# Last tiles in groups of 256, 128 and 128 tokens, a lane for the MLP's weight sums, and a block inverse in two halves

## The chip, the cores and the metric

One core of a Trainium2 chip runs the whole kernel: TensorE (PE) multiplies, VectorE (DVE), ScalarE (ACT) and GpSimd (POOL) do the rest, SyncE (SP) and ScalarE issue the transfers. The metric is device time in microseconds. Each engine works off its own queue in order; an instruction waits there for the data or the buffer it needs, and what stands behind it waits too.

## The reference

Two layers over 512 tokens of width 1024, in float32. Each is `x += mixers(rmsnorm(x) @ w_in) @ w_out` with four mixers (retention, a gated linear recurrence, latent attention, gated DeltaNet), then cross attention on a memory, then the MLP. A final norm ends it:

```python
h = rmsnorm(x, norm_mlp[l])
x = x + jnp.square(jax.nn.relu(h @ mlp_w1[l])) @ mlp_w2[l]
...
return rmsnorm(x, final_norm)
```

The DeltaNet mixer solves a unit lower triangular system of 64 x 64 per chunk and head:

```python
sol = lax.linalg.triangular_solve(lower + jnp.eye(c, dtype=F32), rhs,
                                  left_side=True, lower=True, unit_diagonal=True)
```

## The kernel before

`x` stays on the chip, transposed: eight tiles `xr[m]` of 128 features by 512 tokens. Nearly every large product is split into three: a factor is rounded to a float32r high part (`...h`) by ScalarE, VectorE subtracts to get the low part (`...l`), and PE adds high by high, high by low and low by high in PSUM.

A scheduler orders each engine's queue by a running priority number; `lane(key, base)` (line 212) issues what is inside it with a priority counted on from `base`, or from where that lane was left. The in-projection and the four mixers run in such lanes, from `(2l+1)*1e7 + 1e5` on; what follows the mixers starts at `(2l+1)*1e7 + 5e6` (`end`, line 536). PSUM has two banks under `pj`, two under `gd`, three under `ch` and one under `lg`.

**Weights** come through `wload` (line 276), one unit ahead of another as buffers permit. Most are loaded as `wr` and split into `wh` and `wl`. The units of the MLP's first matrix are treated otherwise: it is multiplied block by block with seven products instead of eight, on sums and differences of its blocks. `wload` brings the four raw blocks (`sr`, two buffers), POOL forms four combinations (`sm`, two buffers), ScalarE rounds three raw blocks (`ah`) and the combinations (`wh`), VectorE makes the low parts `al` (128 x 768, line 299) and `wl` (128 x 1024, line 303). `al` and `wl` have two buffers each, `ah` and `wh` three. Raw buffer `sr` is free once the sums, `ah` and `al` have read it.

**The MLP** combines the normed input in the same way: `prep` forms block differences of `hp`, on VectorE for the last index and on POOL for others, and `combo` splits them into `cxh` and `cxl` (VectorE, line 234). `sprod` (line 1520) runs a weight unit against them in two passes (`dj`), 21 matmuls of 256 columns in each; a pass begins with products on `ah` and `al`, then come those on `wh` and `wl`. Of the first eighth of the hidden width all four units are run, then second-matrix units are interleaved; each fills four PSUM banks, which `evac` (line 1574) empties: VectorE multiplies by the token scale into `t_` (two buffers), POOL adds `t_` to `x`.

**The block inverse** (lines 739 to 790, in the lane `GDN`) inverts 16 pairs of 64 x 64 blocks. VectorE transposes 32-row blocks (lines 763, 764) and four products of 32 small matmuls (`tiles`) follow, each into a `gd` bank; what lies between is a masked product on VectorE, ScalarE copies and two transposes (line 782). Projection matmuls (`pj`) stand between in PE's queue.

**The last tiles** (`last_tiles`, line 1317) end the second layer: the final four feature tiles m = 4 to 7 are computed for two groups of 256 tokens, 12 matmuls each. `tile` adds to `x`, squares it and accumulates; `rstd_of` sums over features with one-column matmuls, `rsqrt1` takes the root (ScalarE, then VectorE with one correction step); `finish` broadcasts the result over the partitions through PE (`bc`) and multiplies eight tiles, five on VectorE and three on POOL, each followed by its output transfer, on ScalarE's queue for odd m and on SP's for even m.

Of the kernel before, what the change touches and what calls it, by code (L numbers as in the profile page):

```python
# [20 lines left out]
S = 512  # L21
# [159 lines left out]
def build(tc, A, out, dbg=None):  # L181
# [10 lines left out]
    def nm(s):  # L192
        uid[0] += 1
        return f"{s}_{uid[0]}"
# [82 lines left out]
    def wload():  # L277
# [7 lines left out]
        if PLAN[i][2][2] is None:  # L285
            sw = wstate["sw"]
            raw = sw.tile([128, n], F32, tag="sr", name=nm("sr"), bufs=2)
            SP.dma_start(out=raw, in_=A["wu"][off:off + 128 * n].rearrange("(p n) -> p n", p=128))
            sm = sw.tile([128, 1024], F32, tag="sm", name=nm("sm"), bufs=2)
            a11, a12, a22, a21 = (raw[:, j * 256:j * 256 + 256] for j in range(4))  # L290
            s1, s3, s2, s4 = (sm[:, j * 256:j * 256 + 256] for j in range(4))
            tt(G, s1, a21, a22, AD)
            tt(G, s2, s1, a11, SU)
            tt(G, s4, a12, s2, SU)
            tt(G, s3, a11, a21, SU)
            ah = sw.tile([128, 768], F32R, tag="ah", name=nm("ah"), bufs=3)
            al = sw.tile([128, 768], F32R, tag="al", name=nm("al"), bufs=2)
            act(ah, raw[:, 0:768], AF.Copy)
            tt(V, al, raw[:, 0:768], ah.bitcast(F32), SU)
            hi = wp.tile([128, n], F32R, tag="whi", name=nm("wh"), bufs=3)  # L300
            lo = wp.tile([128, n], F32R, tag="wlo", name=nm("wl"), bufs=2)
            act(hi, sm, AF.Copy)
            tt(V, lo, sm, hi.bitcast(F32), SU)
            wstate["tiles"][u] = (ah, al, hi, lo)
            return
# [70 lines left out]
    def rsqrt1(o, v, n):  # L376
        w = tiny.tile([128, n], F32, tag=f"rw{n}", name=nm("rw"))
        nv = tiny.tile([128, n], F32, tag=f"rn{n}", name=nm("rn"))
# [54 lines left out]
    def rstd_of(acc, ntt=TT, root=rsqrt, new=None):  # L433
# [5 lines left out]
        v = tiny.tile([128, ntt], F32, tag=f"rv{ntt}", name=nm("rv"))  # L439
        ts(V, v, ps[:, 0:ntt], 1.0 / D, MU, EPS, AD)  # L440
        r = tiny.tile([128, ntt], F32, tag=f"rstd{ntt}", name=nm("rstd"))
# [85 lines left out]
    def layer(l):  # L527
# [111 lines left out]
        def gdn_pre():  # L639
# [121 lines left out]
            for q in range(4):  # L761
                rw, cb = slice(32 * q, 32 * q + 32), slice(32 * (q % 2), 32 * (q % 2) + 32)
                V.transpose(U3[rw, :, cb].rearrange("p t (f r) -> p r f t", f=2), Us3[rw])
                V.transpose(Ta[rw, :, cb], U3[rw, :, cb])
            ps = sct()
            tiles(sb4(ps), N3, cut4(Ta)[:, :, :, 0, :])
            tt(V, cut4(PI)[:, :, :, 0, :], sb4(ps),
               C("zm").unsqueeze(1).unsqueeze(3).to_broadcast([128, 16, 2, 16]), MU)
# [5 lines left out]
            ps = sct()  # L774
            tiles(sb4(ps), PI, cut4(U3)[:, :, :, 1, :])
            act(cut4(U3)[:, :, :, 1, :], sb4(ps), AF.Copy)
# [3 lines left out]
            for p in range(2):  # L780
                ra = slice(64 * p, 64 * p + 32)
                V.transpose(Tb3[ra], U3[ra, :, 0:32])
            ps = sct()
            tiles(sb3(ps), N3, Tb3)
            for p in range(2):
                rb = slice(64 * p + 32, 64 * p + 64)
                act(P1[rb, :, 0:32], sb3(ps)[rb], AF.Copy)
            ps = sct()
            tiles(sb3(ps), P1, U3[:, :, 32:64])
            act(U3[:, :, 32:64], sb3(ps), AF.Copy)  # L790
# [526 lines left out]
        def last_tiles(facc, hh, hl, r2):  # L1317
            ws = [wnext("w27bk0"), wnext("w27ck0")]
            rs, sqs = {}, [None]
            parts = lambda g: [facc[:, g * 256:g * 256 + 256], sqs[0][:, 0:256], sqs[0][:, 256:512]]  # L1320

            def tile(g, m):
                s = slice(g * 256, g * 256 + 256)
                wh, wl = ws[(m - 4) // 2]
                ps = cyb()[:, 0:256]
# [3 lines left out]
                t_ = mp.tile([128, S], F32, tag="t_", name=nm("th"), bufs=2)[:, 0:256]  # L1329
# [3 lines left out]
                sq = sqs[0][:, 256:512] if m == 7 else sqs[0][:, 0:256]  # L1333
# [7 lines left out]
            def finish(g):  # L1341
                s = slice(g * 256, g * 256 + 256)
                b, bp = bcast(rs[g], 256, mp, True)
# [7 lines left out]
            for m in range(4, 8):  # L1351
                tile(0, m)
            p0 = parts(0)
            tile(1, 4)
            rs[0] = rstd_of(p0, 2, rsqrt1)
            tile(1, 5)
            tile(1, 6)
            tile(1, 7)
            rs[1] = rstd_of(parts(1), 2, rsqrt1)
            finish(0)  # L1360
            finish(1)

# [368 lines left out]
```

## Time and profile before

| what | value |
|---|---|
| median of 3 runs | 1622.28 us (1620.12 to 1623.71) |
| the profiled execution's own time | 1620.33 us |
| its span | 1618.5 us |
| PE busy | 1574.2 us, 97% of the span |
| DVE busy | 1134.7 us, 70% |
| ACT busy | 784.2 us, 48% |
| POOL busy | 502.2 us, 31% |
| granted PE clock, mean | 0.992 of full speed |

The span runs from the first to the last instruction of the one profiled execution. Busy shares are means over stages that differ; starts in a timeline are counted from the start of the span. PEclk is the granted TensorE clock as a share of 2.4 GHz, so 0.5 is 1.2 GHz. In a timeline row the number in brackets is the idle time before the instruction and what ended it. A plain float32 matmul appears as two records, a float32r one as one.

### The profile page before, as it was taken

The page shows a single profiled execution, that of the slowest core. Times are in us where ns is not written, and L with a number is a line of the kernel's source. Part 1 is how long each engine was busy: PE and PEld are TensorE (multiplying, and loading weights), DVE is VectorE, ACT ScalarE, POOL GpSimd, SP SyncE. Part 2 cuts the span into 40 slices and gives each one's busy share as a digit, 9 for nine tenths or more (in the row PEclk, how much of TensorE's full clock was granted, in tenths as well). Part 3 has the DMA queues.
Part 4 walks back from the last instruction along what each step waited for, and adds up shares of the span by engine and source line. Part 5 has one row for each costly group of instructions (what it writes and reads, how often), then busy time and mean ns, then how long its engine had stood idle before and what let it go on. Part 6 is the DMA issues. An engine that isn't in the chain of part 4 may idle for free.

```text
span 1618.5 us, 25948 instructions
## 1 busy us (share of the span) xinstructions
PE 1574.2 (97%) x10094; PEld 1366.5 (84%) x10094; DVE 1134.7 (70%) x2197; ACT 784.2 (48%) x1269; POOL 502.2 (31%) x473
## 2 busy tenths in 40 slices
PE   9999999999999999999999999999999899999997
PEld 7768898888888998889886788988888889999886
DVE  7887786456577666766787968745576777766665
ACT  5655654344454444444445656434355544444434
POOL 0100000201274566665301000002014665565543
PEclk9999999999999999999999999999999999999998
DMA  5211125332213223232331212253322223232321
GB/s 184 76 52 54 46 74 167 129 116 80 91 66 105 102 94 97 99 104 66 124 117 48 66 41 75 94 168 117 105 65 92 92 92 104 93 105 93 104 66 65
DMA packets 48074, 150.81 MB, mean 93 GB/s; under 512 B 5712, under 2 KB 9808, under 8 KB 47952
## 3 DMA queue, kind: packets, MB, share of 16 engines
q1 hardware_dynamic: 46800, 148.12, 27.8%
q8 instruction: 79, 1.29, 0.3%
q10 hardware_dynamic: 1152, 1.05, 0.2%
q14 instruction: 43, 0.35, 0.1%
HBM read 144.95 MB, written 4.19 MB: 92 GB/s over the span
## 4 chain that ended last, share of the span: by engine, by line
PE 74%; DVE 13%; issue 4%; ACT 3%; POOL 3%; DMA 3%; SPq 0%; POOLq 0%; DVEq 0%; ACTq 0%
PE ch L249 25%; PE pj L249 23%; PE gd L249 18%; PE lg L249 7%; DVE wl L234 2%; DMA wr<-in_wu 2%; POOL hp L234 1%; PE ch L454 1%; ACT wh L246 1%; POOL sm L234 1%; POOL acc L234 1%; DVE x L234 1%; DMA mem<-in_memT 1%; DVE Pm L241 0%; ACT hp L246 0%
## 5 line engine op out<-in xcount | busy, mean ns | idle before, releaser
L234 DVE TENSOR_TENSOR wl<-wr,wh 128x1024 fp32r<-128x1024 f32 (+2 forms) x193 | 257.5, 1334 | 228.8 <-issue 74.1
L246 ACT ACTIVATE wh<-wr 128x1024 fp32r<-128x1024 f32 (+2 forms) x193 | 201.4, 1044 | 252.9 <-DMA wr<-in_wu 74.8
L249 PE MATMUL ch<-hp,wh 128*128 128x512 f32 (+1 forms) x768 | 238.4, 392 | 0.9 <-DVE hp L234 0.9
L234 POOL TENSOR_TENSOR sm<-sr 128x256 f32<-128x256 f32 x128 | 99.7, 800 | 343.4 <-PE pj L249 133.4
L249 PEld LDWEIGHTS ch<-hp,wh 128*128 128x128 f32 x768 | 140.4, 189 | 29.3 <-DVE hp L234 1.5
L249 PE MATMUL ch<-hp,wl 128*128 128x512 f32 (+1 forms) x384 | 150.4, 392 | 0.0
L234 POOL TENSOR_TENSOR acc<-acc,sq 128x512 f32<-128x512 f32 x33 | 52.9, 1603 | 299.5 <-ACT sq L246 299.5
L246 ACT ACTIVATE wh<-sm 128x1024 fp32r<-128x1024 f32 x64 | 67.4, 1053 | 124.9 <-PE lg L249 110.7
L234 DVE TENSOR_TENSOR al<-sr,ah 128x768 fp32r<-128x768 f32 x64 | 89.4, 1397 | 50.4 <-PE gd L249 50.3
L246 ACT ACTIVATE W<-W 128x1024 f32<-128x1024 f32 x64 | 67.7, 1059 | 80.0 <-DVE W L234 79.1
L249 PE MATMUL pj<-wl,xh 128*128 128x256 f32 (+1 forms) x352 | 106.5, 303 | 0.0
L249 PE MATMUL pj<-wh,xl 128*128 128x256 f32 (+1 forms) x352 | 104.5, 297 | 0.0
L249 PE MATMUL pj<-wh,xh 128*128 128x256 f32 (+1 forms) x352 | 103.0, 293 | 1.4 <-DVE gd L237 1.3
L249 PE MATMUL pj<-cxh,wl 128*128 128x256 f32 x360 | 102.5, 285 | 0.4 <-DVE wl L234 0.4
L249 PE MATMUL pj<-cxh,wh 128*128 128x256 f32 x360 | 102.1, 284 | 0.0
L249 PE MATMUL pj<-cxl,wh 128*128 128x256 f32 x360 | 101.4, 282 | 0.0
L249 PEld LDWEIGHTS ch<-hp,wl 128*128 128x128 f32 x384 | 72.4, 189 | 16.1
L234 DVE TENSOR_TENSOR wl<-sm,wh 128x1024 fp32r<-128x1024 f32 x64 | 80.3, 1254 | 4.0 <-PE gd L249 2.9
L249 PE MATMUL lg<-hp,wh 128*128 128x512 f32 (+1 forms) x256 | 78.9, 390 | 0.0
L246 ACT ACTIVATE ah<-sr 128x768 fp32r<-128x768 f32 x64 | 53.9, 846 | 49.3 <-PE gd L249 37.2
L249 PE MATMUL gd<-cxh,al 128*128 128x256 f32 x240 | 68.4, 285 | 6.2 <-DVE al L234 6.2
L249 PEld LDWEIGHTS pj<-wh,xh 128*128 128x128 f32 x352 | 67.6, 192 | 2.9 <-DVE gd L237 1.8
(789 smaller groups left out, 4673.4 us busy)
## 6 DMA issues: line engine op xcount, KB each, us to landing
wr<-in_wu SPq DMA_DIRECT2D x183, 512.0 KB, 3.4
sr<-in_wu SPq DMA_DIRECT2D x64, 512.0 KB, 3.4
x<-in_xT SPq DMA_DIRECT2D x16, 256.0 KB, 4.0
wr<-in_wu SPq DMA_DIRECT2D x8, 360.0 KB, 2.9
mem<-in_memT SPq DMA_DIRECT2D x16, 128.0 KB, 3.0
xs<-x SPq DMA_DIRECT2D x8, 256.0 KB, 2.3
x<-xs SPq DMA_DIRECT2D x8, 256.0 KB, 2.7
big<-in_wmla SPq DMA_DIRECT2D x2, 640.0 KB, 4.6
```

The lines of the kernel that those rows point to most:

```text
L234: e.tensor_tensor(o, a, b, op=op)
L246: ACT.activation(o, i, f, **k)
L249: PE.matmul(o, lhsT=l, rhs=r, start=st, stop=sp, **k)
L454: PE.transpose(o, i, ident)
```

## The change

Three parts. `wload` puts everything that it does for a unit of the MLP's first matrix into a lane of its own, whose numbers begin where those of the layer's later half begin, so that these instructions go ahead of all others of that half once they are issued. The block inverse runs each of its four products as two halves of eight blocks, each with its own 256-column half bank, and its transposes of line 764 and 782, its ScalarE copies and its masked product in halves too. The last tiles run in token groups of 256, 128 and 128; the middle group has four of its eight closing products on POOL.

```diff
         if PLAN[i][2][2] is None:
+            with lane(f"sw{l}", (2 * l + 1) * 10000000 + 5000000):
+                sw = wstate["sw"]
...
-            def tiles(o, l_, r_):
-                for a in range(16):
+            def tiles(o, l_, r_, h):
+                for a in range(8):
                     for p in range(2):
                         rw = slice(64 * p, 64 * p + 64)
-                        mm(o[rw, a], l_[rw, a, :], r_[rw, a], True, True)
+                        mm(o[rw, a], l_[rw, 8 * h + a, :], r_[rw, 8 * h + a], True, True)
+            def open_(h):
+                for q in range(4):
+                    rw, cb = slice(32 * q, 32 * q + 32), slice(32 * (q % 2), 32 * (q % 2) + 32)
+                    if h == 0:
+                        V.transpose(U3[rw, :, cb].rearrange("p t (f r) -> p r f t", f=2), Us3[rw])
+                    V.transpose(Ta[rw, HV[h], cb], U3[rw, HV[h], cb])
+            def two_(h):
+                ps = sct()[:, 0:256]
+                tiles(sb4(ps), PI, cut4(U3)[:, :, :, 1, :], h)
+                act(cut4(U3)[:, HV[h], :, 1, :], sb4(ps), AF.Copy)
+                for p in range(2):
+                    ra = slice(64 * p, 64 * p + 32)
+                    V.transpose(Tb3[ra, HV[h]], U3[ra, HV[h], 0:32])
...
+            open_(0)
+            one(0)
+            open_(1)
+            one(1)
...
+            for f, h in ((two_, 0), (two_, 1), (three, 0), (three, 1), (four, 0), (four, 1)):
+                f(h)
...
+            GR = ((0, 256), (256, 128), (384, 128))
...
-                    if m in (2, 5, 7):
+                    if m in ((2, 5, 7), (1, 3, 5, 7), (2, 5, 7))[g]:
...
+            for g in range(3):
+                p = parts(g - 1) if g else None
+                tile(g, 4)
+                if g:
+                    root(g - 1, p)
+                for m in range(5, 8):
+                    tile(g, m)
+                if g == 2:
+                    root(2, parts(2))
+                if g:
+                    finish(g - 1)
+            finish(2)
```

The scheduler turns the first part into a few moves. At the opening of the first MLP VectorE's queue stood like this, from the accumulation of squares (`acc`) on; `hp` and `cxl` are the combinations of the input and their low parts, the first `al` and `wl` are of the MLP's fourth unit, the next two of the fifth:

```order
L234 TENSOR_TENSOR acc_4545<-acc_4545,sq_5118 128x512
L234 TENSOR_TENSOR hp_4884<-hp_4883,hp_4884 128x256
L234 TENSOR_TENSOR cxl_4907<-hp_4883,cxh_4906 128x512
L234 TENSOR_TENSOR hp_4884<-hp_4883,hp_4884 128x256
L234 TENSOR_TENSOR cxl_4909<-hp_4883,cxh_4908 128x256
L234 TENSOR_TENSOR cxl_4911<-hp_4884,cxh_4910 128x512
L234 TENSOR_TENSOR al_4934<-sr_4926,ah_4933 128x768
L234 TENSOR_TENSOR cxl_4913<-hp_4884,cxh_4912 128x512
L234 TENSOR_TENSOR wl_4938<-sm_4928,wh_4937 128x1024
L234 TENSOR_TENSOR al_4995<-sr_4987,ah_4994 128x768
L234 TENSOR_TENSOR wl_4999<-sm_4989,wh_4998 128x1024
```

The first `al` stood behind five operations on the input. In the changed kernel, at the same place, VectorE's queue is:

```order
L234 TENSOR_TENSOR acc_4560<-acc_4560,sq_5133 128x512
L234 TENSOR_TENSOR al_4949<-sr_4941,ah_4948 128x768
L234 TENSOR_TENSOR hp_4899<-hp_4898,hp_4899 128x256
L234 TENSOR_TENSOR cxl_4922<-hp_4898,cxh_4921 128x512
L234 TENSOR_TENSOR wl_4953<-sm_4943,wh_4952 128x1024
L234 TENSOR_TENSOR hp_4899<-hp_4898,hp_4899 128x256
L234 TENSOR_TENSOR cxl_4924<-hp_4898,cxh_4923 128x256
L234 TENSOR_TENSOR cxl_4926<-hp_4899,cxh_4925 128x512
L234 TENSOR_TENSOR cxl_4928<-hp_4899,cxh_4927 128x512
L234 TENSOR_TENSOR al_5010<-sr_5002,ah_5009 128x768
L234 TENSOR_TENSOR wl_5014<-sm_5004,wh_5013 128x1024
```

`al` moved to the place behind `acc`, and `wl` ahead of four operations; POOL's queue and PE's are the same here. At the first evacuation of the first MLP VectorE's queue held, from the token scale (`r`) on, four products `t_`, one for each PSUM bank, and then the weights:

```order
L234 TENSOR_TENSOR r_1076_5415<-bc_5413 128x512
L234 TENSOR_TENSOR t__1077_5417<-ch_5279,r_1076_5415 128x512
L234 TENSOR_TENSOR t__1078_5420<-ch_5280,r_1076_5415 128x512
L234 TENSOR_TENSOR t__1079_5423<-ch_5281,r_1076_5415 128x512
L234 TENSOR_TENSOR t__1080_5426<-lg_5282,r_1076_5415 128x512
L234 TENSOR_TENSOR wl_5445<-sm_5435,wh_5444 128x1024
L234 TENSOR_TENSOR al_5532<-sr_5524,ah_5531 128x768
```

The four products stood together. In the changed kernel the weights stand among them on VectorE:

```order
L234 TENSOR_TENSOR r_1080_5430<-bc_5428 128x512
L234 TENSOR_TENSOR t__1081_5432<-ch_5294,r_1080_5430 128x512
L234 TENSOR_TENSOR al_5547<-sr_5539,ah_5546 128x768
L234 TENSOR_TENSOR t__1082_5435<-ch_5295,r_1080_5430 128x512
L234 TENSOR_TENSOR wl_5460<-sm_5450,wh_5459 128x1024
L234 TENSOR_TENSOR t__1083_5438<-ch_5296,r_1080_5430 128x512
L234 TENSOR_TENSOR t__1084_5441<-lg_5297,r_1080_5430 128x512
```

`al` now goes ahead of the second product and `wl` ahead of the third; on POOL two of the four additions of `t_` stand behind three and four sums. This is the only place in an MLP where POOL's queue differs. In layer 0 PE's queue at the second and third product of the inverse (`gd_894`, `gd_932`; `ch` belongs to the attention) was:

```order
L249 MATMUL gd_894<-g_140_841,g_138_799 64x32 x32
L249 MATMUL ch_1491<-bf_194_1229,bf_192_1227 128x256
L454 MATMUL ch_1503<-cst,o_274_1483 128x128 x2
L249 MATMUL ch_1472<-o_276_1489,bf_196_1231 128x128
L249 MATMUL pj_2100<-wl_1980,xh_126 128x256
L249 MATMUL pj_2100<-wh_1979,xl_134 128x256
L249 MATMUL pj_2100<-wh_1979,xh_127 128x256
L249 MATMUL pj_2100<-wl_1980,xh_127 128x256
L249 MATMUL pj_2100<-wh_1979,xl_135 128x256
L249 MATMUL gd_932<-g_145_928,g_132_741 64x32
```

Between the two products stood five projection matmuls and three groups of the attention. In the changed kernel PE's queue has, for the halves of the first (`gd_877`), second (`gd_902`, `gd_922`) and third product (`gd_942`, `gd_961`):

```order
L249 MATMUL gd_877<-g_141_843,g_132_741 64x32
L249 MATMUL gd_902<-g_140_841,g_138_799 64x32 x12
L249 MATMUL gd_877<-g_141_843,g_132_741 64x32 x15
L249 MATMUL gd_902<-g_140_841,g_138_799 64x32 x4
L456 MATMUL ch_1502<-cst,o_270_1479 128x128
L249 MATMUL pj_2115<-wl_1995,xh_126 128x256
L249 MATMUL pj_2115<-wh_1994,xl_134 128x256
L249 MATMUL pj_2115<-wh_1994,xh_127 128x256
L249 MATMUL gd_922<-g_140_841,g_138_799 64x32 x16
L249 MATMUL gd_942<-g_145_900,g_132_741 64x32 x16
L249 MATMUL ch_1506<-bf_198_1244,bf_196_1242 128x256
L249 MATMUL gd_961<-g_145_900,g_132_741 64x32
```

Halves of one product and of the next now stand side by side, and the projection matmuls that stood between them have moved behind. In the last tiles PE's queue has 48 matmuls of 256 columns and 96 of 128 instead of 96 of 256; each group's fourth-tile matmuls stand ahead of the root of the group before. On ScalarE's queue the four transfers of the first group stand ahead of the middle group's square root, and three of the middle group's transfers ahead of the last `bc`.

## Rows read from the trace of the kernel before

**Rows 1.** TensorE's waits: engine, line, releaser, us in total, times, longest
```profile
PE gd L249 <- DVE al L234: 6.2, 2, 3.1
PE gd L249 <- DVE g L764: 3.4, 2, 1.8
```

**Rows 2.** Windows: stretch, length, busy time by engine, PEclk, DMA share, GB/s
```profile
469.60:473.00 3.40, 3.37 (x16) 3.37 (x17) 3.40 (x4) 0.00 (x0) 0.00 (x0) 0.51 0.44 154
926.98:933.80 6.82, 6.82 (x95) 6.53 (x93) 4.58 (x11) 1.73 (x3) 2.25 (x4) 0.51 0.03 9
```

**Rows 3.** Timeline, TensorE, MLP openings: start, us, engine, line, tiles, form, wait
```profile
466.11 0.28 PE L249 MATMUL gd<-cxh,ah 128*128 128x256 f32 x1
466.23 0.28 PE L249 MATMUL gd<-cxl,ah 128*128 128x256 f32 x1
...
469.63 0.58 PE L249 MATMUL gd<-cxh,al 128*128 128x256 f32 x1 [3.12 <-DVE al L234]
...
473.44 0.28 PE L249 MATMUL gd<-cxh,ah 128*128 128x256 f32 x1
...
1266.67 0.39 PE L249 MATMUL gd<-cxh,al 128*128 128x256 f32 x1 [3.12 <-DVE al L234]
...
1270.70 0.41 PE L249 MATMUL gd<-cxh,ah 128*128 128x256 f32 x1
```

**Rows 4.** Timeline, ScalarE, before and in the first MLP
```profile
418.00 0.83 ACT L246 ACTIVATE ah<-sr 128x768 fp32r<-128x768 f32 x1
...
466.92 1.06 ACT L246 ACTIVATE wh<-sm 128x1024 fp32r<-128x1024 f32 x1 [0.83 <-POOL sm L234]
...
509.84 0.85 ACT L246 ACTIVATE ah<-sr 128x768 fp32r<-128x768 f32 x1 [1.79 <-PE gd L249]
```

**Rows 5.** Timeline, VectorE, opening of the first MLP
```profile
464.19 1.23 DVE L234 TENSOR_TENSOR acc<-acc,sq 128x512 f32<-128x512 f32 x1
465.35 0.96 DVE L234 TENSOR_TENSOR hp<-hp,hp 128x256 f32<-128x256 f32 x1
...
468.63 0.94 DVE L234 TENSOR_TENSOR al<-sr,ah 128x768 fp32r<-128x768 f32 x1
...
470.11 1.21 DVE L234 TENSOR_TENSOR wl<-sm,wh 128x1024 fp32r<-128x1024 f32 x1
```

**Rows 6.** Timeline, VectorE, first evacuation of the first MLP
```profile
509.46 0.69 DVE L234 TENSOR_TENSOR t__1077_5417<-ch,r 128x512 f32<-128x512 f32 x1
...
513.42 1.69 DVE L234 TENSOR_TENSOR wl<-sm,wh 128x1024 fp32r<-128x1024 f32 x1
```

**Rows 7.** Timeline, TensorE, the third bank after that evacuation
```profile
513.97 0.62 PE L249 MATMUL ch<-hp,wh 128*128 128x512 f32 x2
514.43 0.39 PE L249 MATMUL ch<-hp,wl 128*128 128x512 f32 x1
```

**Rows 8.** Timeline, TensorE, products of the inverse, layers 0 and 1
```profile
148.39 2.05 PE L249 MATMUL gd<-g,g 64*64 64x32 f32 x62
...
926.68 3.48 PE L249 MATMUL gd<-g,g 64*64 64x32 f32 x62 [1.80 <-DVE g L764]
```

**Rows 9.** Timeline, VectorE, transposes of the inverse in layer 0
```profile
146.44 1.43 DVE L782 STREAM_TRANSPOSE g<-g 32x512 f32<-32x512 f32 x2
```

**Rows 10.** Timeline, TensorE, last tiles
```profile
1599.20 0.47 PE L249 MATMUL gd<-hp,wh 128*128 128x256 f32 x1
...
1604.85 0.28 PE L249 MATMUL gd<-hp,wl 128*128 128x256 f32 x1
...
1610.03 1.19 PE L249 MATMUL gd<-cst,rstd 128*128 128x128 f32 x4 [2.42 <-DVE rstd L237]
```

**Rows 11.** Timeline, TensorE, plain float32 matmuls of 128 columns
```profile
199.92 2.84 PE L249 MATMUL ch<-o,bf 128*128 128x128 f32 x24
```

**Rows 12.** Timeline, POOL, last products
```profile
1611.79 2.09 POOL L234 TENSOR_TENSOR x<-x,bc 128x256 f32<-128x256 f32 x3 [2.83 <-ACT bc L246]
```

**Rows 13.** Timeline, ScalarE, its last transfers
```profile
1613.23 1.96 ACTq L1349 DMA_DIRECT2D out<-x  x4
```

More of the change, by code (lines that the diff above doesn't have):

```diff
@@ L285, in wload @@
         if PLAN[i][2][2] is None:
[L286 to L303, printed above, removed]
+            with lane(f"sw{l}", (2 * l + 1) * 10000000 + 5000000):
+                sw = wstate["sw"]
+                raw = sw.tile([128, n], F32, tag="sr", name=nm("sr"), bufs=2)
+                SP.dma_start(out=raw, in_=A["wu"][off:off + 128 * n].rearrange("(p n) -> p n", p=128))
+                sm = sw.tile([128, 1024], F32, tag="sm", name=nm("sm"), bufs=2)
+                a11, a12, a22, a21 = (raw[:, j * 256:j * 256 + 256] for j in range(4))
+                s1, s3, s2, s4 = (sm[:, j * 256:j * 256 + 256] for j in range(4))
+                tt(G, s1, a21, a22, AD)
+                tt(G, s2, s1, a11, SU)
+                tt(G, s4, a12, s2, SU)
+                tt(G, s3, a11, a21, SU)
+                ah = sw.tile([128, 768], F32R, tag="ah", name=nm("ah"), bufs=3)
+                al = sw.tile([128, 768], F32R, tag="al", name=nm("al"), bufs=2)
+                act(ah, raw[:, 0:768], AF.Copy)
+                tt(V, al, raw[:, 0:768], ah.bitcast(F32), SU)
+                hi = wp.tile([128, n], F32R, tag="whi", name=nm("wh"), bufs=3)
+                lo = wp.tile([128, n], F32R, tag="wlo", name=nm("wl"), bufs=2)
+                act(hi, sm, AF.Copy)
+                tt(V, lo, sm, hi.bitcast(F32), SU)
             wstate["tiles"][u] = (ah, al, hi, lo)
@@ L376, in rsqrt1 @@
     def rsqrt1(o, v, n):
[L377 to L378 removed]
+        w = tiny.tile([128, 2], F32, tag="rw2", name=nm("rw"))[:, 0:n]
+        nv = tiny.tile([128, 2], F32, tag="rn2", name=nm("rn"))[:, 0:n]
         act(o, v, AF.Sqrt)
@@ L438, in rstd_of @@
                 mm(ps[:, t:t + 1], a[:, t * 128:(t + 1) * 128], ones, i == 0, i == len(accs) - 1)
-        v = tiny.tile([128, ntt], F32, tag=f"rv{ntt}", name=nm("rv"))
+        n2 = max(ntt, 2)
+        v = tiny.tile([128, n2], F32, tag=f"rv{n2}", name=nm("rv"))[:, 0:ntt]
         ts(V, v, ps[:, 0:ntt], 1.0 / D, MU, EPS, AD)
-        r = tiny.tile([128, ntt], F32, tag=f"rstd{ntt}", name=nm("rstd"))
+        r = tiny.tile([128, n2], F32, tag=f"rstd{n2}", name=nm("rstd"))[:, 0:ntt]
         root(r, v, ntt)
@@ new lines, in one @@
+            def one(h):
+                ps = sct()[:, 0:256]
+                tiles(sb4(ps), N3, cut4(Ta)[:, :, :, 0, :], h)
+                tt(V, cut4(PI)[:, HV[h], :, 0, :], sb4(ps),
+                   C("zm").unsqueeze(1).unsqueeze(3).to_broadcast([128, 8, 2, 16]), MU)
+            def two_(h):
+                ps = sct()[:, 0:256]
+                tiles(sb4(ps), PI, cut4(U3)[:, :, :, 1, :], h)
[3 more added lines that the diff above has]
+                    V.transpose(Tb3[ra, HV[h]], U3[ra, HV[h], 0:32])
@@ new lines, in three, with four @@
+            def three(h):
+                ps = sct()[:, 0:256]
+                tiles(sb3(ps), N3, Tb3, h)
+                for p in range(2):
+                    rb = slice(64 * p + 32, 64 * p + 64)
+                    act(P1[rb, HV[h], 0:32], sb3(ps)[rb], AF.Copy)
+            def four(h):
+                ps = sct()[:, 0:256]
+                tiles(sb3(ps), P1, U3[:, :, 32:64], h)
+                act(U3[:, HV[h], 32:64], sb3(ps), AF.Copy)
+            open_(0)
+            one(0)
+            open_(1)
@@ L1349, in finish, with root @@
                     (ACT if m % 2 else SP).dma_start(out=out[:, m, s], in_=xr[m][:, s])
[L1351 to L1361, printed above, removed]
+            def root(g, p):
+                rs[g] = rstd_of(p, GR[g][1] // 128, rsqrt1)
+            for g in range(3):
[10 more added lines that the diff above has]
+            finish(2)
         pv = [[bank("lg"), cht()], []]
```

40 lines of the change are left out of this document (11 added, 29 removed).

## The prediction

> **What bounds the kernel now.** I read the busy shares first: TensorE is busy nearly the whole span, so a stage is worth what TensorE idles or runs slowly in it. The list of its waits says where the three edits touch that. The largest entry is TensorE waiting for `al`, the low part of a raw MLP weight, 6.2 us in two waits of at most 3.1; the second is its wait for the transposes of line 764 in the block inverse, 3.4 us in two waits [rows 1]. Each is one wait per layer. Then the windows: after such waits the granted clock is 0.51, the lower of the two levels, for 3.4 us at the first MLP opening and for 6.8 us in the second layer's inverse [rows 2]. Work done there takes twice as long, so these stretches lose about 1.7 and 3.3 us beside the waits. Last I read the timelines of the places, engine by engine.
>
> **MLP openings, the lane.** In layer 0 TensorE issues a 256-column matmul every 0.12 us, stops after 466.23 and goes on at 469.63, when `al` is there [rows 3]. The inputs of that `al` are old: its `ah` was rounded at 418.00 [rows 4]. VectorE came to it late because the accumulation at 464.19 was followed by the combinations and their low parts, and `al` only began at 468.63 [rows 5]. In the new order it stands right behind the accumulation, so it may begin where 465.35 stands. What does it cost there? POOL still sums until ScalarE's `wh` can begin at 466.92 [rows 4], and beside POOL a 256-column operation took 0.96 us, while `al`'s 768 columns took 0.94 with POOL idle [rows 5], some 0.3 to 0.4 per 256. Beside POOL, then, `al` runs at about 0.4 of its pace: in the 1.55 us to 466.9 some 0.7 of it is done, the rest takes 0.25, and it ends at 467.1. TensorE needs it at 466.35, so 0.75 us of the 3.12 stays.
>
> The next thing late is `wl`, the low part of the same unit's sums. Ahead of it now stand one combination (0.4) and one low part of 512 columns (0.7, from the same pace), so it starts at 468.2, just after `wh` (467.98, [rows 4]), and with its 1.21 [rows 5] ends at 469.4. TensorE reaches it nine matmuls after 467.15, at 468.2, and waits 1.2. Ten more matmuls bring it at 470.6 to the second pass over the columns, which began at 473.44: 2.8 us earlier. In layer 1 the wait is the same 3.1 [rows 1] and that pass began at 1270.70 [rows 3]. Carried over by the start of the late matmul (1266.67 there, 469.63 here, hence 797.04 later), the new start is 1267.6: 3.1 earlier. Together **-5.9**. It includes that two short waits instead of a long one leave the clock alone; if it falls all the same, each opening gives 1.7 back. If TensorE meets neither wait the gain is 7.8, and if it meets both and the `wl` of the next unit is late too, it is about 2. Raw weight buffers also come free earlier, as `al` is their last reader, so the following units' transfers start some 2 us sooner, and I expect no new wait for them.
>
> **The first evacuation in each MLP.** The same lane puts an `al` behind the first of the four `t_` products and a `wl` behind the second. Before, the four stood together from 509.46 and `wl` followed at 513.42 [rows 6]; TensorE took the third bank at 513.97 [rows 7] without a wait. Now `al` can't begin before its `ah` ends at 510.69 [rows 4]. With POOL adding to `x` beside it I price `al` and `wl` at 1.69 each, as that `wl` cost [rows 6]: 512.4, second product until 513.0, `wl` until 514.7, third product until 515.3. TensorE is queued behind the third bank, and everything behind it: +1.3 per layer, **+2.6** (0 if both are done in clear time, 4.6 if the two take 2.2 each). Two of the four additions on POOL also move behind three and four sums; their results are not read until the next evacuation, some 10 us on, so I price that at nothing. Without that cover it is one 0.7 us product per layer.
>
> **The block inverse in halves.** The same products are issued, in two PSUM banks of half the width. A half takes 1.05 us at the full clock, from 2.05 for a whole one in layer 0 [rows 8]. The first wait is barely touched: the transposes of line 763 stay whole, and only those of line 764 between them are halved, four at 0.7 (the shape of line 782's, 1.43 for two, [rows 9]), so the first product can start at most 1.4 us sooner. I take 1.0 of it in each layer. In layer 1 the product that follows ran at the half clock, 3.48 us for 62 [rows 8], and the stretch loses 3.3 us. I give the shorter wait three chances in ten to keep the clock, another 1.0. That makes **-3.0**. The bound on the good side is -5.3 (both waits 1.0 shorter, clock kept). On the bad side: a hand-off between two products is two transposes and a ScalarE copy. The transposes take 0.7 when halved, and beside them runs the other half product with 1.05; that leaves 0.35 for the copy, just enough for 256 columns, and in layer 0 the new order has only three projection matmuls besides. If each of six halves in two layers waits 0.4 and layer 0 loses its clock once as well, it is +4.8 and +3.4.
>
> **The last tiles.** The second group of 256 tokens becomes two of 128, so 84 matmuls of 128 columns stand where 36 of 256 ran from 1599.20 to 1605.1 [rows 10]. No row shows a rounded matmul of 128 columns. From below, by columns alone, it costs half of 0.12, from above the plain float32 ones with 128 columns give (2.84-0.28)/23 = 0.11 each [rows 11]; two such records make one plain float32 product, which gives 0.22 if the rounded form were to lose its advantage in narrow tiles. I take 0.11, the nearest row: 9.2 us, and 0.7 for the first two broadcasts and sums, so the last weight matmul ends near 1609.9 instead of 1605.1, +4.8. What follows is shorter. The last group's product, addition and square lose some 0.13 each (0.4), the sums over three pieces are for one token tile (0.5), four VectorE products between reciprocal and rstd are narrower (0.6), the broadcast takes half of its 1.19 us [rows 10], three POOL products at 0.70 come to about 0.45 (0.7, [rows 12]), VectorE's five take 0.6 less, of which half shows, and the last bytes are half as many (0.4 of the 3.3 us between ScalarE's last issue and the end, [rows 13]). Together -3.5. ScalarE now issues three transfers ahead of the last `bc`, 0.49 each [rows 13], and four ahead of the middle group's square root; most passes while VectorE works, and I leave +0.3 (0 to 1.5). Sum **+1.6**, from -3.4 with the low price to +4.3 with the other bounds.
>
> The Trainium skill, "TensorE: Matmul & The Clock Gate", section "Back-to-back issue gap", gives a sustained 81 ns per matmul at 128 columns, which would make the 84 cost 6.8 and the whole sum 2.4 lower. The same sentence has 131 ns at 512 columns, where the trace shows 0.62-0.39 = 0.23 [rows 7], so I let the trace decide.
>
> **Sum.** -5.9 + 2.6 - 3.0 + 1.6 = -4.7. The profiled execution took 1620.33 us (span 1618.5), which makes 1615.6; it lies 1.95 under the median of the runs, so I predict **1617.6**.
>
> **Rivals.**
> *The clock falls anyway.* Two waits of about one us, close together, may do what one of three did: +3.4 at the openings, and the inverse gives only 1.0 of its 3.0. Sum +0.7, time 1623.0. For it: the clock also fell after waits of 1.8 us [rows 2, 8]. Against: each wait is shorter than that.
> *The lane moves nothing that counts.* POOL's order at the openings is unchanged, and if a sum on POOL is what really comes last, the 6.2 us stay while the evacuations pay 2.6: +1.2, 1623.5. Against: the trace names `al`, and its inputs were ready some 47 us before.
> *Narrow matmuls at the plain float32 price* (slower): 84 at 0.22 instead of 0.11 is +9.2 more, sum +4.5, 1626.8. It decides from about 0.17 us per matmul, where the other terms are used up. For it: every 128-column matmul in the trace is plain float32, so none shows otherwise. Against: 256 columns cost half of 512, with no floor in sight.
> *The halves starve TensorE*: +8.2 in the place of -3.0, sum +6.5, 1628.8. It needs a wait of 0.4 at every half.
> *Narrow matmuls are cheap and the inverse keeps its clock*: -3.4 and -5.3 for +1.6 and -3.0, sum -12.0, 1610.3.
>
> **Chances.** Forecast 0.43, clock 0.18, lane idle 0.06, narrow price 0.12, starving halves 0.09, both cheap 0.12. Each has some 3 us of its own to either side. About 0.2% (3.2 us) is what a measurement of this kernel tells from no change. Of the forecast three quarters lie below 1619.1 (0.33); with the cheap case and a little of the clock's (0.05) that is faster 0.50. The rest of the forecast (0.10), most of the clock and lane cases (0.17) and some of the narrow price (0.04) make same 0.31; the others slower 0.19. Range 1609.5 to 1626: it takes in the cheap case and most of the narrow price, and leaves out the starving halves. The forecast's own range is 1614.5 to 1620.5.
>
> **What would show it.** Right: at the MLP openings TensorE's wait for `al` under 1 us, a new one for `wl` of about 1, the clock at its upper level; a new wait of about 1.3 us in `ch` for the third `t_` product; 128-column matmuls 0.11 apart; the last broadcast some 1 us later than before. Wrong: the 3.1 us waits unchanged, waits for ScalarE copies or line 782's successors between halves, or 0.2 us and more between narrow matmuls.

## The result, and the profile after

The changed kernel takes 1629.53 us (median of 7 runs, 1623.84 to 1631.88), the kernel before 1619.97 in the same 7 rounds: ratio 1.0062, interval [1.0046, 1.0077]. It is slower by 0.6%, where I had forecast 1617.6, faster than before, and a range up to 1626.

The profiled execution of the changed kernel is its shortest: 1623.84 us, span 1622.0, against 1620.33 and 1618.5. I walked through both by landmarks on TensorE, each the first or last matmul of a kind, and noted by how much the changed kernel is ahead (-) or behind:

| landmark | before | after | lag |
|---|---|---|---|
| first MLP, first product | 455.18 | 453.56 | -1.62 |
| its fourth unit, second pass [rows 3] | 473.44 | 469.18 | -4.26 |
| its sixth weight unit | 492.90 | 491.26 | -1.64 |
| layer 1, first `gd<-g,g` | 919.49 | 917.15 | -2.34 |
| second MLP, first product | 1252.24 | 1245.04 | -7.20 |
| second MLP, sixth unit | 1289.41 | 1282.16 | -7.25 |
| last tiles, first matmul of 256 columns | 1588.66 | 1581.39 | -7.27 |
| last tiles, last weight matmul | 1604.85 | 1611.03 | +6.18 |

Up to the last tiles this execution is 7 us ahead; how much of that is this one execution's luck is told under the experiments. The last tiles then cost 13.4 us more on TensorE. That is the first thing to read, in the windows of the changed kernel (stretch, length, busy time of PE, PEld, DVE, ACT and POOL, PEclk, DMA share, GB/s):

```profile
1588.00:1592.80 4.80, 3.13 (x26) 2.85 (x26) 2.58 (x9) 4.65 (x9) 0.00 (x0) 1.00 0.00 0
1592.80:1611.20 18.40, 18.40 (x88) 18.40 (x88) 7.48 (x31) 5.44 (x18) 2.11 (x3) 0.50 0.17 57
```

The clock falls at 1592.8. It fell in the same place before, and came back; the same columns of the kernel before:

```profile
1599.40:1602.80 3.40, 3.40 (x17) 3.40 (x17) 1.47 (x7) 1.22 (x4) 0.00 (x0) 0.51 0.00 0
1602.80:1605.00 2.20, 2.20 (x22) 2.20 (x20) 1.79 (x8) 1.52 (x4) 0.00 (x0) 1.00 0.00 0
```

In the changed kernel it doesn't come back, though TensorE is busy in 18.40 of 18.40 us. What a narrow matmul costs on either side of the fall is in TensorE's timeline (a row with x2 and the `wl` behind it are three matmuls):

```profile
1592.30 0.38 PE L249 MATMUL gd<-hp,wh 128*128 128x128 f32 x2
1592.63 0.47 PE L249 MATMUL gd<-hp,wh 128*128 128x128 f32 x2
...
1596.31 0.63 PE L249 MATMUL gd<-hp,wh 128*128 128x128 f32 x2
1596.95 0.63 PE L249 MATMUL gd<-hp,wh 128*128 128x128 f32 x2
```

The first three take 0.33 us at the upper level, 0.11 each as I had priced them. Four us later three take 0.64, or 0.213 each. 84 at that price are 18 us. My sign of being wrong, "0.2 us and more between narrow matmuls", came true. The mean granted clock was low in all seven runs of the changed kernel, 0.986 to 0.989; in 29 runs of the kernel before (below) it was 0.988 to 0.995.

The tail behind the last weight matmul did become shorter. The last group's broadcast starts at 1615.43, 4.4 us after that matmul (before 5.2, [rows 10]), and ScalarE then copies it and issues the last four transfers (its timeline):

```profile
1616.27 0.28 ACT L246 ACTIVATE bc<-gd 128x128 f32<-128x128 f32 x1 [1.67 <-DMA out<-x]
1617.52 1.85 ACTq L1375 DMA_DIRECT2D out<-x  x4
```

From the last weight matmul to the end it is 11.0 us, before 13.7.

At the MLP openings the changed waits are the ones I forecast, and one more. TensorE's waits in the changed kernel (releaser, us in total, times, longest), against [rows 1]:

```profile
PE gd L249 <- DVE W L234: 3.6, 2, 2.2
PE gd L249 <- DVE g L770: 3.2, 2, 1.7
PE pj L249 <- DVE wl L234: 2.6, 2, 1.3
PE gd L249 <- DVE al L234: 0.8, 2, 0.4
```

The wait for `al` is 0.4 per layer instead of 3.1 and a new one for `wl` takes 1.3 (I had 0.75 and 1.2). The first row is new: TensorE waits for `W`, the additions that empty the first unit's PSUM banks. In its timeline the three stand at the first opening like this:

```profile
465.28 0.39 PE L249 MATMUL gd<-cxh,al 128*128 128x256 f32 x1 [0.38 <-DVE al L234]
...
467.88 0.39 PE L249 MATMUL pj<-cxh,wl 128*128 128x256 f32 x1 [1.28 <-DVE wl L234]
...
479.80 0.39 PE L249 MATMUL gd<-cxh,ah 128*128 128x256 f32 x1 [2.22 <-DVE W L234]
```

Where the 2.22 us come from is told by POOL and ScalarE, which feed `W`. POOL's timeline, then ScalarE's:

```profile
469.08 2.64 POOL L234 TENSOR_TENSOR sm<-sr 128x256 f32<-128x256 f32 x2 [3.27 <-DMA sr<-in_wu]
471.68 1.72 POOL L234 TENSOR_TENSOR sm<-sm,sr 128x256 f32<-128x256 f32 x1
473.47 1.33 POOL L234 TENSOR_TENSOR sm<-sr,sm 128x256 f32<-128x256 f32 x1
```

```profile
474.83 1.06 ACT L246 ACTIVATE wh<-sm 128x1024 fp32r<-128x1024 f32 x1 [4.99 <-POOL sm L234]
475.80 0.36 ACT L246 ACTIVATE p<-gd 128x256 f32<-128x256 f32 x1
```

The raw weights of the fifth unit came 4.1 us earlier than before, 2.5 of it beyond the stage's own lead (I had some 2), but POOL now sums them beside VectorE's `al` and `wl`: 5.7 us for the four sums, where before they took 3.5 (473.21 to 476.75). ScalarE waits 4.99 us for them with `wh`, and `p`, which `W` needs, stands behind `wh` in ScalarE's queue. So `p` comes only 1.95 us earlier than before, and the stage itself had started 1.62 earlier: of the 2.6 us won nearly all are given back. Behind this wait the granted clock fell too, as the window shows:

```profile
480.00:483.50 3.50, 3.50 (x18) 3.50 (x18) 3.46 (x6) 3.47 (x4) 3.04 (x2) 0.51 0.46 133
```

By what I counted for such a fall, that is another 1.7 us at this opening; some of the two losses is made up before the sixth unit, where the kernel before had a wait of 0.92 us for `hp` (at 487.44) that the changed one has not. In the second layer -7.20 becomes -10.04 and then -7.25, with a wait of 1.40 for `W` and no fall of the clock.

### The profile page after: what moved, and what is told of

Same layout as the page of the kernel before. It is cut to its first block, busy times and chain, and to the rows that moved or that the text cites. A ratio compares the mean times of both kernels' runs of the same rounds, so it can differ in the third digit from the quotient of the medians.

```text
span 1622.0 us, 26130 instructions
## 1 busy us (share of the span) xinstructions
PE 1582.6 (98%) x10142; PEld 1376.4 (85%) x10142; DVE 1140.1 (70%) x2231; ACT 786.5 (48%) x1287; POOL 507.9 (31%) x477
## 3 DMA queue, kind: packets, MB, share of 16 engines
q8 instruction: 79, 1.29, 0.3%
## 4 chain that ended last, share of the span: by engine, by line
PE 75%; DVE 11%; issue 5%; ACT 4%; POOL 4%; DMA 2%; SPq 0%; POOLq 0%; DVEq 0%; ACTq 0%
PE ch L249 25%; PE pj L249 23%; PE gd L249 18%; PE lg L249 8%; DVE wl L234 2%; POOL hp L234 1%; POOL sm L234 1%; PE ch L456 1%; DMA wr<-in_wu 1%; ACT wh L246 1%; POOL acc L234 1%; DVE x L234 1%; DVE g L769 0%; DVE W L234 0%; DVE Pm L241 0%
## 5 line engine op out<-in xcount | busy, mean ns | idle before, releaser
L249 PE MATMUL ch<-hp,wh 128*128 128x512 f32 (+2 forms) x792 | 245.8, 392 | 1.0 <-DVE hp L234 1.0
L249 PEld LDWEIGHTS ch<-hp,wh 128*128 128x128 f32 x792 | 146.7, 193 | 29.4 <-DVE hp L234 1.3
L249 PE MATMUL ch<-hp,wl 128*128 128x512 f32 (+2 forms) x396 | 155.4, 392 | 0.0
L249 PEld LDWEIGHTS ch<-hp,wl 128*128 128x128 f32 x396 | 76.4, 193 | 16.2
L249 PE MATMUL lg<-hp,wh 128*128 128x512 f32 (+2 forms) x264 | 81.4, 391 | 0.0
L249 PE MATMUL gd<-cxh,ah 128*128 128x256 f32 x240 | 67.9, 283 | 3.7 <-DVE W L234 3.6
L249 PEld LDWEIGHTS pj<-cxh,wl 128*128 128x128 f32 x360 | 68.6, 191 | 3.0 <-DVE wl L234 3.0
```

What stands on the lines that cost most here:

```text
L249: PE.matmul(o, lhsT=l, rhs=r, start=st, stop=sp, **k)
```

## The experiments

Each was timed beside the kernel before, on the same chip as it; the first four, the next four and the last two kernels ran on three chips, so where kernels of different batches are compared the ratios to the kernel before are the better measure. Beside the first four kernels 29 runs of the kernel before spread from 1613.9 to 1627.2, median 1618.97; beside the next four its median is 1618.86, beside the last two 1619.01.

**The parts one by one.** The first four kernels take each part alone or one away. Each edit is a whole piece of the diff shown above; a line or two stand for it here.

The changed kernel with the tail of before:

```diff
-            GR = ((0, 256), (256, 128), (384, 128))
...
+                s = slice(g * 256, g * 256 + 256)
```

> Lane and halves as in the changed kernel, the last tiles as before. Theory A (the 128-column groups cost the time: TensorE runs them at the lower clock, which never comes back): from the first 256-column matmul of the last tiles to the last weight matmul about 16 us as before instead of 29.6, the time 6 to 8 us under before. Rival B (the lane or the halves cost it, and the last tiles were worth about what I forecast): within 2 us of the changed kernel, some 8 us over before.

The kernel before with the three token groups, nothing else:

```diff
+            GR = ((0, 256), (256, 128), (384, 128))
...
+            for g in range(3):
```

> The kernel before with the last tiles of 256, 128 and 128 alone. Theory A: 10 to 13 us slower than before, the clock at 0.5 from the middle group to the end. Rival B: at most 2 us slower.

The kernel before with the lane:

```diff
+            with lane(f"sw{l}", (2 * l + 1) * 10000000 + 5000000):
```

> The kernel before with the lane alone. Theory A: within 2 us of before: some 2.7 us won at each MLP opening and given back within 13 us as a wait of TensorE for W, because POOL's sums, slowed by VectorE, hold ScalarE's wh and behind it p. My forecast: 3.3 us faster. Rival B: 5 us or more slower.

The kernel before with the inverse in halves:

```diff
+            for f, h in ((two_, 0), (two_, 1), (three, 0), (three, 1), (four, 0), (four, 1)):
+                f(h)
```

> The kernel before with the inverse in halves alone. Theory A: 4 to 6 us faster, nearly all in layer 1, where the clock stays at its upper level after the first product. My forecast: 3.0 us faster. Rival B: not faster, the halves wait for each other.

| kernel | median us | ratio to before, interval |
|---|---|---|
| old tail (lane and halves) | 1617.18 | 0.9992 [0.9978, 1.0005] |
| tail only | 1631.83 | 1.0074 [1.0052, 1.0096] |
| lane only | 1617.23 | 0.9991 [0.9977, 1.0006] |
| halves only | 1618.53 | 0.9999 [0.9980, 1.0017] |

The last tiles alone cost 12.9 us by the medians, and without them the changed kernel is no different from before. The two ratios multiply to 1.0066, the whole change has 1.0062. Theory A holds for the tail: TensorE takes 29.71 us from the first 256-column matmul of the last tiles to the last weight matmul with the tail alone, 16.17 with the old tail, and the mean granted clock was 0.985 to 0.987 in all six runs of the tail alone, below all 29 runs of the kernel before beside them. For the size of the rest theory A was wrong: I expected 6 to 8 us from lane and halves and 4 to 6 from the halves, read off the one profile, and neither shows in the runs. The window of the narrow groups in the run with the tail alone, and the place of the fall:

```profile
1593.00:1598.00 5.00, 3.34 (x28) 3.05 (x27) 2.26 (x8) 4.20 (x9) 0.62 (x1) 1.00 0.00 0
1599.00:1617.00 18.00, 18.00 (x86) 18.00 (x86) 7.31 (x30) 5.04 (x15) 2.11 (x3) 0.50 0.17 59
```

18 us at 0.50 with TensorE busy throughout.

Why the profile of the changed kernel showed a gain of 5 us in layer 1 and the runs don't is seen in the profiles of all kernels. Windows from 905 to 950 us, around the second inverse, of the kernel without halves but with wide narrow groups (below), and of the one with lane and halves:

```profile
905.00:950.00 45.00, 42.14 (x510) 36.10 (x508) 35.48 (x74) 22.96 (x47) 3.46 (x6) 1.00 0.17 59
```

```profile
905.00:950.00 45.00, 42.13 (x478) 36.94 (x478) 33.86 (x74) 21.42 (x44) 3.46 (x6) 0.89 0.17 56
```

The clock held without the halves and fell with them. Over the twelve profiles it held in two of the four with halves and in two of the eight without. Six of these eight kernels issue the same instructions, in the same order on each engine, until the last tiles; of them the clock held in two and fell in four. So whether it holds there differs from execution to execution, and one profile of each kernel can't price a part by it. Of the 4.9 us that the changed kernel's profile gains in layer 1, 3.2 are this fall, and 1.2 are two waits for the weights of the cross attention, at 1062 and 1063 us, that the profile of before shows and most of the others don't. The halves' own wait hardly changed: 3.2 us in two waits, before 3.4.

**What keeps the clock low.** The narrow groups differ from the wide ones in the width of each matmul and in the number of roots and waits. The next kernel keeps everything but the width:

```diff
-                ps = cyb()[:, 0:w]
+                ps = cyb()[:, 0:256]
+                s2 = slice(256, 512) if g else s
-                    mm3_cm(ps, wh[:, c], wl[:, c], hh[k][:, s], hl[k][:, s], k == 0, k == 3)
+                    mm3_cm(ps, wh[:, c], wl[:, c], hh[k][:, s2], hl[k][:, s2], k == 0, k == 3)
+                ps = ps[:, s.start - s2.start:s.stop - s2.start]
```

> As the run with the last tiles alone (256, 128, 128 on the kernel before), but each matmul of the two narrow groups computes 256 columns, of which 128 are used: the same number of matmuls, waits and roots. Theory A1 (the stream of 128-column matmuls is too light to bring the clock back, the fall itself comes from the wait before it): the clock rises some 3.4 us after it fell, the matmuls go 0.12 apart, and the time is 5 to 7 us under that of the narrow groups though twice the columns are computed. Rival A2 (the three roots and their waits keep the clock low, whatever the width): the clock stays at 0.5 and the time is that of the narrow groups.

It took 1621.02 us, ratio 1.0016 [1.0001, 1.0030]: twice the columns in the same matmuls, and 10.8 us less than the narrow ones by the medians, 9.4 by the ratios. That is more than the 5 to 7 I expected. Its windows:

```profile
1590.00:1594.40 4.40, 3.11 (x24) 2.64 (x23) 2.58 (x9) 4.25 (x9) 0.00 (x0) 1.00 0.00 0
1595.00:1597.80 2.80, 2.80 (x15) 2.80 (x15) 1.45 (x8) 0.98 (x4) 0.00 (x0) 0.50 0.00 0
1598.40:1606.30 7.90, 7.90 (x70) 7.90 (x69) 5.40 (x23) 3.21 (x10) 2.12 (x3) 1.00 0.39 134
```

The clock falls after the same wait, stays down some 3.4 us and comes back. A1 holds for this half, and it is the width, not the waits, that decides whether the clock comes back. How soon it does is no constant either: in the kernel with `p` on VectorE (below), whose last tiles are those of before, the clock stayed down 6.6 us and more behind the same wait:

```profile
1594.40:1601.00 6.60, 6.60 (x31) 6.60 (x32) 2.39 (x10) 3.49 (x7) 0.00 (x0) 0.50 0.00 0
```

And in the profile with the lane alone, again with the tiles of before, it didn't fall there at all.

**Can the narrow stream keep the clock?** The next kernel fills TensorE's wait before the narrow groups with matmuls whose results are overwritten:

```diff
+                if (g, m) == (1, 4):
+                    for r in range(2):
+                        for k in range(4):
+                            c = slice(k * 256, k * 256 + 128)
+                            mm3_cm(pw[:, 0:256], wh[:, c], wl[:, c], hh[k][:, 256:512], hl[k][:, 256:512], k == 0, k == 3)
```

> As the run with the last tiles alone, with 24 more matmuls of 256 columns (results overwritten) in TensorE's wait for the first root, so that it doesn't idle before the narrow groups. If the narrow stream can't raise the clock but can keep it: clock 1.0 through the middle group, 128-column matmuls 0.11 apart, 6 to 9 us faster than the narrow groups alone. If the narrow stream itself lets the clock fall: it falls some us later all the same, and the gain is under 3 us.

1628.23 us, ratio 1.0048 [1.0029, 1.0067], 3.6 under the tail alone by the medians, with intervals that overlap; it fits neither expectation. Its windows:

```profile
1590.00:1597.40 7.40, 7.40 (x65) 7.40 (x64) 5.09 (x13) 4.94 (x11) 2.65 (x2) 1.00 0.01 2
1597.40:1598.80 1.40, 1.40 (x16) 1.40 (x14) 0.29 (x1) 1.38 (x2) 0.00 (x0) 1.00 0.00 0
1599.20:1618.50 19.30, 19.30 (x92) 19.30 (x92) 7.71 (x33) 5.49 (x17) 2.10 (x3) 0.50 0.17 56
```

TensorE is never idle there and the clock falls at 1599 all the same. By itself this would say that the narrow stream lets it fall. But ahead of the fall stood not only 12 narrow matmuls, also the first root's sums, 12 records of one column (the second row, which counts some of their neighbours too). So another filling of 24 was put behind those sums, with only this edit:

```diff
-                if (g, m) == (1, 4):
+                if (g, m) in ((1, 4), (1, 5)):
```

> As the run with the filled wait, with another 24 matmuls of 256 columns behind the first root's one-column matmuls, so that the narrow stream starts from 2.9 us of dense work. If the narrow stream by itself lets the clock fall (theory A1): it falls within the 60 narrow matmuls that follow without a wait, these go from 0.11 to 0.21 apart, and the time is some 2 us over that of the single filling. If the one-column matmuls of the root made it fall: the clock stays at 1.0 until the second root at least, and the time is 2 us or more under that of the single filling in spite of the added work.

1623.59 us, ratio 1.0034 [1.0020, 1.0049]: 4.6 us under the single filling by the medians, with 24 matmuls more. By the ratios it is 2.3 us, and their intervals overlap, so the times alone don't settle it. The profiles say more: from the first 256-column matmul of the last tiles to the last weight matmul TensorE took 24.50 us here, 30.82 with the single filling. And the mean granted clock of the runs averages 0.992 over the ten of this kernel and 0.988 over the six of the single filling. The windows of the double filling:

```profile
1592.60:1594.00 1.40, 1.40 (x16) 1.40 (x14) 0.29 (x1) 1.38 (x2) 0.00 (x0) 1.00 0.00 0
1594.00:1596.90 2.90, 2.90 (x25) 2.90 (x26) 1.22 (x8) 1.06 (x4) 0.00 (x0) 1.00 0.00 0
1596.90:1607.40 10.50, 10.50 (x96) 10.46 (x94) 5.49 (x23) 3.22 (x10) 2.11 (x3) 1.00 0.27 90
```

The whole narrow stream, 10.5 us with the second root's sums in it, ran at 1.00 and in TensorE's timeline at 0.11 per matmul to its end:

```profile
1606.67 0.38 PE L249 MATMUL lg<-hp,wh 128*128 128x128 f32 x2
1607.01 0.39 PE L249 MATMUL lg<-hp,wh 128*128 128x128 f32 x2
```

My theory A1 falls in this part. At the upper level the narrow stream keeps the clock; at the lower level it doesn't bring it back, in 18 us with the tail alone and 19.3 with the single filling. In the single filling it fell behind the stretch of one-column sums; with 24 more matmuls behind that stretch it held. So the narrow stream alone is not what makes it fall. Nor are the sums alone: the second root's sums stand inside the narrow stream here, and in the next kernel the first root's stand between matmuls of 256 columns, and in both the clock held. What made it fall in the single filling, sums and narrow matmuls together or the chance of that execution, is not shown. The 48 filling matmuls are 5.9 us themselves at 0.12, less some 1.7 that stand in waits, so of the 4.6 us by which this kernel is over the kernel before most is the fillings' own time: by this estimate narrow groups at the upper level would cost little, as forecast for them.

**The same filling before.**

```diff
+                if (g, m) == (1, 4):
+                    for r in range(2):
+                        for k in range(4):
+                            c = slice(k * 256, k * 256 + 128)
+                            mm3_cm(ps, wh[:, c], wl[:, c], hh[k][:, s], hl[k][:, s], k == 0, k == 3)
```

> The kernel before with the same 24 matmuls in TensorE's wait for the first root. The clock doesn't fall at that place (0.51 for 3.4 us before); the matmuls of the last group end about 1.7 us sooner, less some 0.5 by which the extra ones delay the root: 0 to 1.5 us faster than before. If the fall has another cause than the idle time: no change, or slower by what is added.

1618.66 us, ratio 1.0000 [0.9984, 1.0015]. The clock held, as its window shows:

```profile
1598.50:1604.20 5.70, 5.70 (x52) 5.70 (x50) 3.61 (x14) 3.19 (x8) 0.00 (x0) 1.00 0.00 0
```

From the first 256-column matmul of the last tiles to the last one TensorE took 15.57 us instead of 16.19. That is 0.6 us of the 1.5 that I had set as the upper end, and too little to tell by the runs. In the old last tiles the clock held in both profiles with the wait filled (here and in the last kernel below); with the wait left open it held in one of five. That fits the idle time as the cause of the fall, but these are few executions.

**What the opening's gain was lost to.** This kernel has the lane and the halves, the old tail, and `p` copied by VectorE in the first eighth of the MLP; the additions into `W` also go ahead of other work, by a lane of their own that is not in the lines shown:

```diff
-                act(p1, blk(bk[3], 0), AF.Copy)
+                if e == 0:
+                    V.tensor_copy(p1, blk(bk[3], 0))
+                else:
+                    act(p1, blk(bk[3], 0), AF.Copy)
```

> Lane and halves, last tiles as before, and the copy p of the first eighth of the MLP on VectorE instead of behind wh on ScalarE (the additions W first as well). Theory (the opening's gain is given back because p waits behind wh, and wh for POOL's sums): TensorE's wait for W at the openings, 2.2 and 1.4 us, falls by at least half, and the layer's MLP start keeps 1 to 2 us of the 2.7 that are won at each opening; time 2 to 4 us under the version without it. Rival (TensorE waits for the sums' own wl a little later anyway): a wait for wl or al takes its place and the time stays.

1617.85 us, ratio 0.9993 [0.9979, 1.0006]; without it 1617.18. TensorE's waits in it:

```profile
PE gd L249 <- DVE g L769: 5.0, 3, 1.7
PE pj L249 <- DVE wl L234: 2.5, 2, 1.3
PE gd L249 <- DVE W L234: 0.2, 1, 0.2
```

The wait for `W` fell from 2.3 us in the same kernel without this edit to 0.2, so the queue in front of it, `p` behind `wh` and `W` behind other work, was its cause; which of the two edits did it was not tried apart. The time did not follow. In the first opening of this execution the clock fell after the wait for `wl` (0.80 and 0.78 in the two stretches of 4 us from 465.5 on), and in the second the lag went from -3.26 at the first product to -6.10 at the fourth unit's second pass and back to -4.07 at the sixth unit. How much of the openings' gain is kept can't be settled with differences of 1 us: from first product to sixth unit, in the profiles with the lane and without this edit, a layer keeps between 0.0 and 0.7 against the profile of before. What the lane does change is the clock. Without it the clock fell in all 14 openings of the seven profiles, at the wait for `al`; with it in 3 of 10: here, in the kernel that follows (0.51 from 1265.2 on, in its second opening), and behind the wait for `W` in the changed kernel.

**A candidate.** The lane and the filled wait together, no halves, old tail:

```diff
+            with lane(f"sw{l}", (2 * l + 1) * 10000000 + 5000000):
...
+                if (g, m) == (1, 4):
+                    for r in range(2):
```

> A candidate: the kernel before with the lane and the filled wait in its old last tiles of 256, no halves. The lane alone came out 1.7 us under before and the filling alone 0.2 under, both within what can be told. If they add up: 1 to 3 us under before; rival: no difference.

1617.53 us, ratio 0.9993 [0.9978, 1.0007]. Nothing that I tried beats the kernel before by more than can be told.

## Why the prediction was wrong

The step that failed is the price of the narrow matmuls in the last tiles. I took "0.11, the nearest row: 9.2 us" for the 84 of them. The single price was right, 0.11 at the upper clock level. What I left out is that the stretch where they would run was one where the clock had just fallen: the row that I used for its start, 1599.20 with 0.47 us [rows 10], is itself a slow one, and the windows of before had 0.51 from there on. The sum has no term for the clock in the last tiles; I put it at nothing, without a reason. In fact the loss depends on what runs in it. A stream of 256 columns got the clock back in 3.4 us, before and in the kernel with the wide groups, and within 7 us in every profile whose last tiles are 256 columns wide; the stream of 128 columns did not in any of the three profiles in which it met the lower level (18.4, 18.0 and 19.3 us), and each matmul took 0.213 instead of 0.11 to the end. The term is 13.4 us on TensorE instead of 4.8, and with the shorter end behind it 10.8 instead of 1.6 in the profile, 12.9 by the medians of the part alone.

A row of mine had spoken of it. The stretch at half clock in the second inverse lasted 6.8 us [rows 2], twice that of the MLP opening, and its first half is the 3.48 us of small products [rows 8]; it ended 3.7 us after the projection's 256-column matmuls had begun at 930.09. I read it only as a loss of 3.3 us, not as a sign that small products may not bring the clock back. It was a hint at most: in the kernel with `p` on VectorE the clock stayed down as long behind the last tiles' first wait, with 256 columns in each weight matmul.

Two of my rivals gave nearly the right time by luck, each by another mechanism. Narrow rounded matmuls at the price of plain float32 ones, 1626.8, are refuted in the double filling, where they cost 0.11 throughout. The starving halves, 1628.8, are refuted by the kernel with the halves alone, which is no slower than before.

The MLP openings, -5.9: mechanism and sizes were right at the place, 2.6 and 2.8 us won at the second pass where I had 2.8 and 3.1. But I followed the chain only to that pass, and of the units behind it I wrote that I expected no new wait. The next wait, for `W` behind `p` and `wh` and POOL's sums, gave back what was won, all of it in the profile of the changed kernel. The lane alone is 0.9991 [0.9977, 1.0006], a gain between 3.7 us and nothing. I had weighed POOL against VectorE only for `al`, not for the sums that POOL does at the same time.

The first evacuations, +2.6: under 0.1 us in each layer. `al` was not held up beside POOL (VectorE's timeline of the changed kernel):

```profile
508.36 0.95 DVE L234 TENSOR_TENSOR al<-sr,ah 128x768 fp32r<-128x768 f32 x1
...
511.47 0.68 DVE L234 TENSOR_TENSOR t__1083_5438<-ch,r 128x512 f32<-128x512 f32 x1
```

It took 0.95 us where I had 1.69, and the third product ended at 512.15; TensorE came to its bank at 512.24, 0.23 us behind the matmul before it, as without a wait. The `wl` between them cost 1.73, as priced. What I had not priced is POOL's side: its two additions beside them took 1.95 and 2.28 us instead of 1.29. At the opening it was POOL's sums again that became slower. I had put the price of the clash on VectorE alone.

The inverse, -3.0: 0.9999 [0.9980, 1.0017] by itself. I took 1.0 us off the first wait in each layer; it became shorter by 0.1 (1.61 to 1.54, and 1.80 to 1.69). At the first inverse the clock fell in three of the four profiles with halves, the changed kernel's among them (3.5 us from 128.4 on), and in four of the eight without. Most of the gain in the profile is the clock's, which holds or falls there with and without the halves. Whether they make the clock hold more often is left open: two of four against two of eight says nothing.

Four figures of the prediction don't follow from its own terms. From 1599.20, 9.2 and 0.7 us lead to 1609.1, +4.0, not to 1609.9 and +4.8; the other 0.8 has no term. The low price takes 84 times 0.05, or 4.2, off the +1.6, which gives -2.6 where I wrote -3.4, and makes the cheap rival 1611.1 and not 1610.3. The upper end of +4.3 I can't get from the bounds given: the transfers' 1.5 leads to +2.8. And an opening that meets neither of two waits of 0.75 and 1.2 is 1.95 better in each layer, so the gain would be 9.8, not 7.8. None of the four is near the 12.9 us that the last tiles cost.

The Trainium skill says in "TensorE: Matmul & The Clock Gate", section "What's actually happening", that TensorE goes to the upper clock after sustained activity. The trace agrees for streams of 256 columns (3.4 us at 0.51 before, 6.6 at 0.50 with `p` on VectorE, then 1.00) and not for those of 128: with the tail alone TensorE is busy in 18.00 of 18.00 us by the records, and the clock stays at 0.50.

## What to carry to other kernels

Before making matmuls narrower, look at the granted clock where they will run. If a wait or a stretch of tiny matmuls stands ahead of them, price the narrow stream at the lower level to its end, and compare it with the wide stream, if rows show that it comes back. When a wait is removed, follow the chain past the next wait on each engine that it speeds up: an earlier start for one pair of engines is a new clash for another. And before reading a gain of a few us off one profile, see whether a fall of the clock in a stretch that the change touches also comes and goes in other executions.

## What the runs showed that I had not expected

A stream of 128-column float32r matmuls, each with its own 128 x 128 weights, ran 0.11 us apart at the upper level and held it for 10.5 us in the one profile that shows it, but at the lower level it ran 0.213 apart and did not raise it in 19.3 us of unbroken work. The double width cost nothing at that level: 256 columns took 0.213 there as well (1599.4 to 1602.8 before). So at the lower level the second 128 columns came free, and the wider matmul is the one that got out.
